# Where the gated-linear-attention levels, the weight folds of the first sub-block and the final norm stand among the projection matmuls of a one-core decoder step

## The chip, the core and the metric

The kernel runs on one core of a Trainium2 chip. The metric is the device time of one launch in microseconds (us); below it is better. The time before is 2868.98 us, the median of three runs between 2868.82 and 2869.27 us. The engines are called PE (matrix), PEld (its weight load), DVE (vector), ACT (scalar functions), POOL (GpSimd) and SP (which issues the DMAs).

## The reference, cut to what matters

One layer of a hybrid decoder is applied to a prompt of 2048 tokens of width 1024 and to 32 sample tokens (8 requests of 4), all in 32-bit floats:

```
q, k, v, r, a, u, sv = split(rmsnorm(x) @ w_in)
logg  = log_sigmoid(a @ w_alpha*rstd + b_alpha) / 16
o, S  = gated linear attention(q, k, v, logg)      # causal, per-channel decay exp(sum of logg)
o     = rmsnorm(o) * silu(r)
s_out = gelu(u) * (causal 128x128 mixing of rmsnorm(gelu(sv)))
h = x + concat(o, s_out) @ w_out
h = h + softmax attention over 256 memory tokens, wq_x and wo_x
y = h + conv_ffn(rmsnorm(h)); final rmsnorm
```

The outputs also hold the states, the memory keys and values and the convolution's last rows.

## The kernel before, in words

The prompt is cut into four sub-blocks of 512 tokens, called s = 0 to 3 here; the 32 sample tokens ride along in s = 1 for the mixer and in s = 2 for the FFN. A product of 32-bit matrices is made of three matmuls on halves that are rounded to a shorter type (`mm3`, lines 92 to 94): ACT makes the high half, DVE the rest (`split`, lines 84 and 85).

**The order of the work** is a list of steps that is written out by hand. `weave` goes through a main list and puts the steps of side lists between its members, spread evenly from a first to a last member. In a mixer the main list is: member 0 the small decay projection, 1 wk, 2 wq, 3 to 6 sv, 7 to 10 v, 11 and 12 u, 13 to 16 r, 17 and 18 the first two parts of w_out. Members 1, 2, 11 and 12 have 48 matmuls of 512 columns with two weight units, the members of sv, v and r 24 matmuls with one weight unit, the two of w_out 24 each. `run` walks the finished list and issues weight loads up to five units ahead of need, all on the SP queue, in the order of the list. The tile framework then orders the instructions of each engine at compile time, by their place in the list and by a simulated schedule; each engine runs its list strictly in that order.

**Marks** number the places between projection matmuls: eight in each 48-matmul member and four in each other one, so that marks 0 to 15 lie in wk and wq, 16 to 31 in sv, 32 to 47 in v, 48 to 63 in u and 64 to 79 in r. `behind(i)` keeps a group of PE instructions behind mark i on PE; it binds PE alone. `step_of(i)` gives the member that holds mark i, and the group's step stands behind that member in the list.

**The gated linear attention** works on two head pairs p = 0 and 1. `gates` (line 967 on) makes the log decays with three ACT functions from two table sets, `cums` sums them on PE. `diag(p)` makes the diagonal of the 128x128 score blocks (eight small ACT copies, line 1022). `level(p, l)`, l = 0 to 6, makes the off-diagonal blocks of size 2^l: DVE subtracts sums (line 1041), ACT takes Exp (lines 1043 and 1046), DVE multiplies with q and k (lines 1053 and 1057), PE makes the scores (line 1064) and DVE copies them in under a mask (line 1068). `decay(p)` and `states(p)` make the running state (line 1126 on PE), `chunks` the outputs (lines 1151 and 1152), `gate`, `times_r` (line 1166) and `back` (line 1223) finish them for w_out. The table `AT` holds the mark of each: levels stand three marks apart, from 18 for p = 0 and from 41 for p = 1.

**ACT** evacuates sv through Gelu (line 887), u through Gelu (line 873) and r through Silu (line 890). Gelu and Exp lie in different table sets, and a change of set is an instruction of its own (ACT_TABLE_LOAD in the profile). The four sv accumulators fill the four banks of the pool `accp`, and v's first matmul needs one of them back.

**The folds** stand in s = 0 alone. `turn_wq` loads 512 KB of wq_x, loads two tiles of a memory key again (`again`, line 585, from four buffers of the tag X, two per turn), transposes wq_x on PE (line 596) and splits it; `fold_qk` multiplies the two (24 matmuls of 256 columns), copies the result (line 619), splits it, makes sums (lines 632 to 635) and writes all of it to DRAM; the writes go onto the SP queue at the next fold (`flush`, line 301). There are eight pairs of turn and fold, 16 steps. `fold_vo` does the like for values and wo_x (8 steps of 12 matmuls of 512 columns, two for each of four heads, which share one reload). The tiles of all this come from the tag U, 49 buffers that the whole mixer shares.

**The final norm** of the sub-block before (`final_steps`, 4 parts, 5 after s = 2: transposes at line 1779, squares at 1780, result at 1786) stands at members 0 and 1 of the next mixer; after s = 2 six steps that write out the convolution rows (line 1797) stand there too.

Of the kernel before, what the change touches and what calls it, by code (L numbers as in the profile page):

```python
# [37 lines left out]
def hymba_step_kernel(  # L38
# [34 lines left out]
    def mps(name):  # L73
        return mmp.tile([128, 512], F32, tag="mm", name=name)
# [390 lines left out]
    def weave(main, *sides):  # L465

        out = []
        due = [0.0] * len(sides)
        at = [0] * len(sides)
        for i, m in enumerate(main):  # L470
            out.append(m)
            for j, (steps, first, last) in enumerate(sides):
                if i < first:
                    continue
                due[j] = len(steps) * min(1.0, (i - first + 1) / (last - first + 1))
                while at[j] < len(steps) and at[j] < due[j] - 1e-9:
                    out.append(steps[at[j]])
                    at[j] += 1
        for j, (steps, _, _) in enumerate(sides):
            out += steps[at[j]:]  # L480
        return out
# [182 lines left out]
    qk_steps = []  # L664
    for h, j in ((2 * i + hh, j) for i in range(2) for j in range(2) for hh in range(2)):
        qk_steps.append(Step(lambda a, h=h, j=j: turn_wq(h, j, a), [wraw_unit(wq_x[0], 4 * j, 4, h * 256, 256, f"wqf{h}{j}")]))
        qk_steps.append(Step(lambda h=h, j=j: fold_qk(h, j)))
    vo_steps = [Step(lambda a, h=h, jh=jh: fold_vo(h, jh, a), [(wo_x[0], 2 * h, 2, jh * 512, 512, f"wof{h}{jh}")])
                for h in range(4) for jh in range(2)]
# [5 lines left out]
    def behind(i):  # L675
        return tc.issue_after(marks[i])
# [227 lines left out]
    def sgu_steps(B):  # L904
# [21 lines left out]
        def mix(h):  # L926
# [22 lines left out]
        return [Step(f) for f in out]  # L949


    AT = {("diag", 0): 17, ("level", 0): 18, ("decay", 0): 39, ("states", 0): 50,
          ("diag", 1): 24, ("level", 1): 41, ("decay", 1): 62, ("states", 1): 66}
    state = {}
    for p in range(2):
        t = cp.tile([128, 128], F32, tag=f"S{p}", name=f"Sz{p}", bufs=2)
# [3 lines left out]
    def gla_steps(B):  # L960
        s, sample = B.s, B.mix_sample
        T = TM if sample else SB
        nt = 5 if sample else 4

        s0_of = {}

        def gates():
            if sample:
# [38 lines left out]
        def diag(p):  # L1007
# [3 lines left out]
            pool.tensor_tensor(pr[:, :T], B.q[p][:, :T], B.k[p][:, :T], ALU.mult)  # L1011
            with behind(AT["diag", p]):
                for c in range(nt):
# [13 lines left out]
        def level(p, l):  # L1027
            half = 1 << l
            Tl = TM if (sample and l < 2) else SB
            nb = Tl // (2 * half)  # L1030

            def lr(t):
                v = t[:, :Tl].rearrange("p (n two h) -> p n two h", two=2, h=half)
                return v[:, :, 0, :], v[:, :, 1, :]


            b3 = B.b[p][:, :Tl].rearrange("p (n w) -> p n w", w=2 * half)
            e = T_(f"e{s}{p}{l}")
            el, er = lr(e)
            if l > 0:  # L1040
                dve.tensor_tensor(e[:, :Tl].rearrange("p (n w) -> p n w", w=2 * half), b3,
                                  b3[:, :, half - 1:half].broadcast_to([128, nb, 2 * half]), ALU.subtract)
                act.activation(el, el, AF.Exp, scale=-1.0)
            else:
                dve.tensor_tensor(er, b3[:, :, 1:2], b3[:, :, 0:1], ALU.subtract)
            act.activation(er, er, AF.Exp)

            kr = T_(f"kr{s}{p}{l}")
            nr = Tl // 2
            kr3 = kr[:, :2 * nr].rearrange("p (hh i) -> p hh i", hh=2)  # L1050
            qr = lr(B.q[p])[1]
            for hh in range(2):
                dve.scalar_tensor_tensor(kr3[:, hh].rearrange("p (n h) -> p n h", h=half),
                                         er, sel[:, hh:hh + 1], qr, ALU.mult, ALU.mult)
            if l > 0:
                kl = e
                dve.tensor_tensor(el, el, lr(B.k[p])[0], ALU.mult)
            else:
                kl = B.k[p]
            ps = mps(f"s{s}{p}{l}")  # L1060
            ps3 = ps.rearrange("p (hh i) -> p hh i", hh=2)
            with behind(AT["level", p] + 3 * l):
                for c in range(4):
                    pe.matmul(ps3[:, :, c * 64:(c + 1) * 64], kl[:, c * 128:(c + 1) * 128],
                              kr3[:, :, c * 64:(c + 1) * 64], start=True, stop=True)
            for hh in range(2):
                dst = B.P[2 * p + hh][:, :SB].rearrange("p (n two h) -> p n two h", two=2, h=half)
                dve.copy_predicated(dst[:, :, 1, :], masks[l].rearrange("p (n h) -> p n h", h=half),
                                    ps3[:, hh].rearrange("p (n h) -> p n h", h=half))
            if sample and l < 2:  # L1070
                ps = mps(f"ss{s}{p}{l}")
                with behind(AT["level", p] + 3 * l):
                    pe.matmul(ps[:NS, :32].rearrange("p (hh i) -> p hh i", hh=2), kl[:, SB:TM], kr3[:, :, 256:272],
                              start=True, stop=True)
                for hh in range(2):
                    dst = B.P[2 * p + hh][:NS, SB:TM].rearrange("p (n two h) -> p n two h", two=2, h=half)
                    dve.copy_predicated(dst[:, :, 1, :], masks[l][:NS, :16].rearrange("p (n h) -> p n h", h=half),
                                        ps[:NS, hh * 16:(hh + 1) * 16].rearrange("p (n h) -> p n h", h=half))

        def decay(p):  # L1080
# [21 lines left out]
            ps = mps(f"ktp{s}{p}")  # L1102
            with behind(AT["decay", p]):
                for c in range(4):
# [4 lines left out]
            if sample:  # L1109
                ps = mps(f"ktps{s}{p}")  # L1110
                with behind(AT["decay", p]):
                    pe.transpose(ps[:NS, :128], kh[:, SB:TM], ident)
# [6 lines left out]
        def states(p):  # L1119

            kv = mps(f"kv{s}{p}")
            with behind(AT["states", p]):
              for c in range(4):
# [129 lines left out]
        put_at(1, lambda: cums(0), lambda: cums(1))  # L1253
        for p in range(2):
            todo = [(AT["diag", p], lambda p=p: diag(p))]
            todo += [(AT["level", p] + 3 * l, lambda p=p, l=l: level(p, l)) for l in range(7)]
            todo.append((AT["decay", p], lambda p=p: decay(p)))
            for i, f in sorted(todo, key=lambda x: x[0]):
                put_at(step_of(i), f)
# [552 lines left out]
    steps = [Step(mem_norm)]  # L1812
    norm = norm_in_steps(blocks[0])
    steps += weave(mem_steps, (norm, 0, 11), ([Step(late_constants)], 2, 2))
    after = []
    for s, B in enumerate(blocks):
        proj = proj_steps(B)
        gla = gla_steps(B)
        sgu_st = sgu_steps(B)
        nst = len(sgu_st) - 4  # L1820
        keep = None
        if B.mix_sample:
            def keep():
                if not hasattr(smp, "x"):
                    smp.x = U("smpx")
                return smp.x
        w1, w2, stat = out_proj_steps(B, lambda k0, m2, s=s: (w_out[0], k0, 4, m2 * 256, 256, f"wo{s}{k0}{m2}"),
                                      lambda B=B: B.cat, "gx", "wo", B.mix_sample, 4, B.mix_sample, keep, seven=True, whole=not B.mix_sample)
        folds = [(qk_steps, 8, 13), (vo_steps, 13, 17)] if s == 0 else []
        steps += weave(proj + w1, *folds, (after, 0, 1),  # L1830
                       *gla,
                       (sgu_st[:1], 6, 6), (sgu_st[1:nst], 7, 8), (sgu_st[nst:], 12, 13))
        scales, sc, turns = attention_steps(B)
        x1, x2, xstat = out_proj_steps(B, lambda k0, m2, s=s: wready(vod[k0 // 4][:, m2], f"wx{s}{k0}{m2}"),
                                       lambda B=B: B.ao, "gffn", "wx", False, 0, B.ffn_sample, seven=s > 0, whole=True)
        steps += w2 + [stat, scales]
        steps += weave(sc + x1, (turns[:2], 8, 9), (turns[2:3], 13, 13), (turns[3:], 14, 14))
        fstart, fmain, flast = ffn_steps(B, s == NSB - 1)
        steps += x2 + [xstat, fstart]
        sides = []  # L1840
        if B.mix_sample:
            sides.append((sample_steps(), 1, len(fmain) - 5))
        if s + 1 == NSB:
            ncs = conv_out_steps(carry, 2, o_state_conv[0, 0], "nc")
            sides.append((ncs[:4], 30, 36))
        steps += weave(fmain[:-4], *sides)
        if s + 1 < NSB:
            after = final_steps(B)
            nxt = blocks[s + 1]
            norm = norm_in_steps(nxt)  # L1850
            if nxt.ffn_sample:
                norm.append(carry_sample(nxt, B))
            steps += weave(fmain[-4:] + flast, (norm, 0, 4))
            if B.ffn_sample:
                after += conv_out_steps(sct, 16, o_state_conv_s[0].rearrange("b t f -> (b t) f"), "ncs")
        else:
            steps += fmain[-4:-2] + flast[:1] + fmain[-2:] + ncs[4:] + flast[1:]
            after = []
# [30 lines left out]
```

## Time and profile before

| what | value |
|---|---|
| median of three runs | 2868.98 us |
| profiled execution, device time | 2865.95 us |
| profiled execution, span from first to last instruction | 2864.2 us |
| PE busy | 2801.3 us, 98% |
| DVE, ACT, POOL busy | 1876.2, 1131.6, 564.4 us |
| mean granted PE clock | 0.992 |

The span is 1.75 us shorter than the device time of the same execution. A row of the windows view gives a stretch, its length, the busy time of each engine in it with the number of instructions, the granted PE clock, the share of the DMA engines and the rate. A row of the timeline gives start, duration, engine, line, operation and tiles, and in brackets the idle time before it with what ended it. A row of the waits gives who waited for whom, the total, how often and the longest one.

### The profile page before, as it was taken

To read this page: it belongs to the slowest core of one execution; us is meant where nothing else is said; L and a number is where in the kernel's file an instruction comes from. 1 tells how busy PE (TensorE), PEld (TensorE's weight loads), DVE (VectorE), ACT (ScalarE), POOL (GpSimd) and SP (SyncE) were. 2 spreads that over 40 slices of the span, in tenths; PEclk is the share of its full clock that TensorE was granted. 3 is DMA by queue.
4 is the path that set the end of the run, shared out by engine and by line. 5 is a ranking of instruction groups with operands and counts; after the bars stand their busy time and mean duration, and the time that the engine had idled before them with its cause. 6 is when DMAs were issued, how large, how long until landed. Compare 5 with 4: busy or idle time off the path is not lost.

```text
span 2864.2 us, 47088 instructions
## 1 busy us (share of the span) xinstructions
PE 2801.3 (98%) x17894; PEld 2478.0 (87%) x17894; DVE 1876.2 (66%) x3262; ACT 1131.6 (40%) x1971; POOL 564.4 (20%) x631
## 2 busy tenths in 40 slices
PE   8988999999999999999999999999999899999998
PEld 8777898888887788998888889899999788899997
DVE  6665768777776676655546767666666677665555
ACT  5544545333356344322224545422223545431222
POOL 2001212111101221321311121222221021132222
PEclk9999999999999999999999999999999999999999
DMA  9355779999952236887886225567776223677775
GB/s 300 108 181 177 272 239 327 338 341 341 319 192 91 82 111 236 299 290 277 315 311 220 81 74 192 201 247 258 258 265 212 86 76 131 215 255 267 272 276 180
DMA packets 369687, 638.21 MB, mean 223 GB/s; under 512 B 27370, under 2 KB 238412, under 8 KB 369462
## 3 DMA queue, kind: packets, MB, share of 16 engines
q1 hardware_dynamic: 369462, 635.20, 65.3%
q8 instruction: 142, 2.33, 0.3%
q14 instruction: 83, 0.68, 0.1%
HBM read 507.69 MB, written 127.41 MB: 222 GB/s over the span
## 4 chain that ended last, share of the span: by engine, by line
PE 87%; DVE 5%; ACT 3%; DMA 2%; issue 2%; POOL 1%; SPq 0%; POOLq 0%; ACTq 0%; DVEq 0%
PE d L92 6%; PE d L94 6%; PE d L93 6%; PE a_wx L92 2%; PE a_wx L94 2%; PE a_wx L93 2%; PE a_wo L92 2%; PE a_wo L93 2%; PE a_wo L94 2%; PE a_wg L94 1%; PE a_wup L94 1%; PE a_wg L92 1%; PE a_wup L93 1%; PE a_wup L92 1%; PE a_wg L93 1%
## 5 line engine op out<-in xcount | busy, mean ns | idle before, releaser
L92 PE MATMUL d<-acth,whi_wd 128*128 128x272 f32 (+1 forms) x688 | 235.6, 342 | 0.0
L94 PE MATMUL d<-acth,wlo_wd 128*128 128x272 f32 (+1 forms) x688 | 233.7, 340 | 0.0
L93 PE MATMUL d<-actl,whi_wd 128*128 128x272 f32 (+1 forms) x688 | 233.7, 340 | 0.0
L1738 DVE TENSOR_TENSOR h<-d,h 128x512 f32<-128x512 f32 (+1 forms) x232 | 133.9, 582 | 147.7 <-PE d L94 147.7
L1640 POOL TENSOR_TENSOR c<-c,bc_f 128x512 f32<-128x512 f32 (+1 forms) x88 | 137.1, 1562 | 138.8 <-ACT c L1639 138.1
L1630 ACT ACTIVATE c<-g,colsb 128x512 f32<-128x512 f32 x88 | 71.7, 815 | 204.5 <-DVE g L1599 154.5
L94 PEld LDWEIGHTS d<-acth,wlo_wd 128*128 128x128 f32 x688 | 129.3, 188 | 15.4 <-issue 1.2
L92 PEld LDWEIGHTS d<-acth,whi_wd 128*128 128x128 f32 x688 | 129.2, 188 | 15.3 <-DVE h L1738 1.7
L93 PEld LDWEIGHTS d<-actl,whi_wd 128*128 128x128 f32 x688 | 129.5, 188 | 13.9 <-issue 0.4
L1662 POOL TENSOR_TENSOR c<-r_q_wup,c 128x512 f32<-128x512 f32 (+1 forms) x33 | 62.7, 1900 | 335.7 <-DVE r_q_wup L286 213.7
L1627 POOL COPY carry<-g 128x2 f32<-128x2 f32 x88 | 30.9, 351 | 434.2 <-DVE g L1599 403.1
L92 PE MATMUL a_wo<-ch,h_wo 128*128 128x512 f32 (+1 forms) x320 | 112.5, 353 | 0.0
L93 PE MATMUL a_wo<-cl,h_wo 128*128 128x512 f32 (+1 forms) x320 | 112.3, 351 | 0.0
L94 PE MATMUL a_wo<-ch,l_wo 128*128 128x512 f32 (+1 forms) x320 | 112.2, 351 | 0.0
L1631 DVE SCALAR_TENSOR_TENSOR c<-g,colsb,c 128x512 f32<-128x512 f32 x88 | 86.1, 978 | 29.0 <-ACT c L1630 28.4
L94 PE MATMUL a_wx<-pTh,wlo_wx 128*128 128x512 f32 x256 | 101.2, 395 | 0.0
L84 ACT ACTIVATE acth<-c 128x512 fp32r<-128x512 f32 (+1 forms) x88 | 55.9, 636 | 113.6 <-DVE c L1662 84.6
L93 PE MATMUL a_wx<-pTl,whi_wx 128*128 128x512 f32 x256 | 100.5, 392 | 0.0
L92 PE MATMUL a_wx<-pTh,whi_wx 128*128 128x512 f32 x256 | 100.3, 394 | 0.0
L1639 ACT ACTIVATE c<-c 128x512 f32<-128x512 f32 (+1 forms) x88 | 56.1, 638 | 103.0 <-DVE c L1632 91.0
L1632 DVE SCALAR_TENSOR_TENSOR c<-g,colsb,c 128x512 f32<-128x512 f32 x88 | 92.7, 1054 | 1.1
L85 DVE TENSOR_TENSOR actl<-c,acth 128x512 fp32r<-128x512 f32 (+1 forms) x88 | 64.3, 733 | 27.2 <-ACT acth L84 26.0
(3757 smaller groups left out, 9731.9 us busy)
## 6 DMA issues: line engine op xcount, KB each, us to landing
whi_wd<-wd SPq DMA_DIRECT2D x66, 512.0 KB, 8.1
wlo_wd<-wd SPq DMA_DIRECT2D x66, 512.0 KB, 7.5
r_wo<-in_w_out_dram SPq DMA_DIRECT2D x32, 512.0 KB, 3.7
wlo_wx<-vod SPq DMA_DIRECT2D x32, 512.0 KB, 4.1
whi_wx<-vod SPq DMA_DIRECT2D x32, 512.0 KB, 5.0
r_wg<-in_w_gate_dram SPq DMA_DIRECT2D x22, 512.0 KB, 7.2
r_wup<-in_w_up_dram SPq DMA_DIRECT2D x22, 512.0 KB, 5.4
r_wd<-in_w_down_dram SPq DMA_DIRECT2D x22, 512.0 KB, 5.2
```

The costliest lines, as they stand in the source:

```text
L84: act.activation(hi, src, AF.Copy)
L85: (lo_eng or dve).tensor_tensor(lo, src, hi.bitcast(F32), ALU.subtract)
L92: pe.matmul(ps, wh, xh, start=first, stop=False)
L93: pe.matmul(ps, wh, xl, start=False, stop=False)
L94: return pe.matmul(ps, wl, xh, start=False, stop=last)
L1630: act.activation(c[:, :SB], g[:, 2:SB + 2], AF.Identity, bias=cb, scale=w2)
L1631: dve.scalar_tensor_tensor(c[:, :SB], g[:, 1:SB + 1], w1, c[:, :SB], ALU.mult, ALU.add)
L1632: dve.scalar_tensor_tensor(c[:, :SB], g[:, 0:SB], w0, c[:, :SB], ALU.mult, ALU.add)
L1639: act.activation(c[:, :T], c[:, :T], AF.Gelu_apprx_tanh)
L1640: pool.tensor_tensor(c[:, :T], c[:, :T], B.fbc[:, :T], ALU.mult)
L1662: (dve, pool)[i].tensor_tensor(c[:, :T], q[i], c[:, :T], ALU.mult)
L1738: dve.tensor_tensor(B.h[m + mm][:, cs], ps[:, :cw], B.h[m + mm][:, cs], ALU.add)
```

## The change

The table of marks becomes two tables, one for s = 0 and one for the other sub-blocks, with a mark of its own for each level. For s = 1 to 3 no level has a mark between 28 and 35 any more; the second pair's diagonal goes from mark 24 to 38 and its states from 66 to 69. For s = 0 all marks are later. The 16 steps of turns and folds of wq_x go from members 8 to 13 to members 0 to 9, the 8 steps for wo_x from 13 to 17 to 10 to 17. The final norm's steps stay at members 0 and 1, but stand behind the gates and the decay sums in the list; the convolution rows after s = 2 go to members 13 to 15.

```diff
-    AT = {("diag", 0): 17, ("level", 0): 18, ("decay", 0): 39, ("states", 0): 50,
-          ("diag", 1): 24, ("level", 1): 41, ("decay", 1): 62, ("states", 1): 66}
+    AT_FOLDS = {("diag", 0): 23, ("level", 0): (24, 27, 36, 39, 42, 45, 48), ("decay", 0): 51, ("states", 0): 56,
+                ("diag", 1): 46, ("level", 1): (52, 55, 58, 61, 64, 67, 70), ("decay", 1): 72, ("states", 1): 73}
+    AT_REST = {("diag", 0): 17, ("level", 0): (18, 21, 24, 27, 36, 38, 40), ("decay", 0): 43, ("states", 0): 50,
+               ("diag", 1): 38, ("level", 1): (45, 47, 50, 53, 56, 58, 61), ("decay", 1): 64, ("states", 1): 69}
...
+        AT = AT_REST if s else AT_FOLDS
...
-            with behind(AT["level", p] + 3 * l):
+            with behind(AT["level", p][l]):
...
-            todo += [(AT["level", p] + 3 * l, lambda p=p, l=l: level(p, l)) for l in range(7)]
+            todo += [(AT["level", p][l], lambda p=p, l=l: level(p, l)) for l in range(7)]
...
-        folds = [(qk_steps, 8, 13), (vo_steps, 13, 17)] if s == 0 else []
-        steps += weave(proj + w1, *folds, (after, 0, 1),
-                       *gla,
+        folds = [(qk_steps, 0, 9), (vo_steps, 10, 17)] if s == 0 else []
+        steps += weave(proj + w1, *folds, *gla, (after[:5], 0, 1), (after[5:], 13, 15),
                        (sgu_st[:1], 6, 6), (sgu_st[1:nst], 7, 8), (sgu_st[nst:], 12, 13))
```

More of the change, by code (lines that the diff above doesn't have):

```diff
@@ L1071, in level @@
                 ps = mps(f"ss{s}{p}{l}")
-                with behind(AT["level", p] + 3 * l):
+                with behind(AT["level", p][l]):
                     pe.matmul(ps[:NS, :32].rearrange("p (hh i) -> p hh i", hh=2), kl[:, SB:TM], kr3[:, :, 256:272],
```

## The prediction

> **What bounds the kernel now.** I read the page first, then the busy time of each engine by stretches, then PE's waits, then the timelines around the two largest.
>
> ```profile
> span 2864.2 us, 47088 instructions
> PE 2801.3 (98%) x17894; PEld 2478.0 (87%) x17894; DVE 1876.2 (66%) x3262; ACT 1131.6 (40%) x1971; POOL 564.4 (20%) x631
> PE 87%; DVE 5%; ACT 3%; DMA 2%; issue 2%; POOL 1%; SPq 0%; POOLq 0%; ACTq 0%; DVEq 0%
> ```
>
> PE is the bound: it sits idle for 2864.2 - 2801.3 = 62.9 us in all. The change adds and removes no matmul, so it can only win idle time and time at a lower clock. The windows say where these are (length, busy PE, PEld, DVE, ACT, POOL, granted clock, DMA share, GB/s):
>
> ```profile
> 76.00:150.00 74.00, 73.51 (x371) 59.67 (x372) 43.63 (x79) 45.54 (x99) 3.93 (x4) 1.00 0.28 87
> 150.00:200.00 50.00, 37.74 (x222) 33.28 (x221) 31.51 (x59) 16.77 (x31) 2.83 (x1) 0.86 0.61 195
> 200.00:240.00 40.00, 38.15 (x234) 32.64 (x233) 22.85 (x43) 16.79 (x27) 0.00 (x0) 1.00 0.54 173
> 240.00:300.00 60.00, 50.80 (x272) 42.94 (x271) 38.71 (x71) 27.27 (x43) 19.73 (x10) 0.89 0.68 223
> 300.00:370.00 70.00, 69.91 (x370) 59.23 (x370) 53.83 (x82) 41.05 (x64) 15.97 (x10) 1.00 0.67 236
> 815.00:1005.00 190.00, 187.32 (x1285) 153.58 (x1284) 130.02 (x276) 92.84 (x189) 32.45 (x27) 1.00 0.26 82
> 1549.00:1715.00 166.00, 164.01 (x891) 137.48 (x891) 112.81 (x200) 86.87 (x161) 26.34 (x19) 1.00 0.28 86
> 2260.00:2300.00 40.00, 32.34 (x164) 27.43 (x164) 29.11 (x58) 28.24 (x77) 5.69 (x3) 0.87 0.23 66
> 2300.00:2385.00 85.00, 85.00 (x479) 72.14 (x479) 57.18 (x98) 36.65 (x48) 17.05 (x11) 1.00 0.24 77
> ```
>
> The mixer of s = 0 (76 to 370) loses the most: 150 to 200 has 50 - 37.74 = 12.3 us idle and, at clock 0.86, up to 50 x 0.14 = 7.0 us of slow running; 240 to 300 has 9.2 us idle and up to 60 x 0.11 = 6.6 us; 200 to 240 has 1.9 us. In s = 3, 2260 to 2300 has 7.7 us idle and up to 40 x 0.13 = 5.2 us. The mixers of s = 1 and 2 lose only 2.7 and 2.0 us, with the clock at 1.00.
>
> What PE waited for in s = 0 (first three rows) and s = 3 (next two), and what the SP queue waited for in s = 0 (last two):
>
> ```profile
> PE qkp L92 <- ACT wqh L84: 12.4, 2, 8.6
> PE t_wr L92 <- ACT h_wr L84: 3.4, 1, 3.4
> PE a_wu L92 <- DVE v L868: 2.7, 1, 2.7
> PE t_wv L92 <- ACT sv L887: 5.7, 1, 5.7
> PE s L1064 <- DVE kr L1053: 1.9, 1, 1.9
> SPq L585 <- PE qkp L94: 47.1, 7, 9.4
> SPq L301 <- ACT qkh L84: 12.8, 5, 4.1
> ```
>
> Two waits of a fold for its split weights make up 12.4 of the 23.4 us that s = 0 loses. Why the split was late, on SP (first two rows) and ACT:
>
> ```profile
> 168.11 1.97 SPq L585 DMA_DIRECT2D kr<-kd  x2
> 170.17 0.38 SPq L102 DMA_DIRECT2D r_wu<-in_w_in_dram  x1
> 174.92 1.06 ACT L84 ACTIVATE h_wu<-r_wu 128x1024 fp32r<-128x1024 f32 x1 [3.44 <-DMA r_wu<-in_w_in_dram]
> 175.88 1.07 ACT L84 ACTIVATE wqh<-wqp 128x512 fp32r<-128x512 f32 x2
> ```
>
> The load of r_wu stands on SP behind the reload of a memory key (line 585), which waits for a fold's last matmul to free its X buffer; ACT runs in order, waits for r_wu, and the fold's split stands behind it. So the folds hold up the projection's loads, and the projection's splits the folds.
>
> In s = 3, on ACT (first four rows) and PE:
>
> ```profile
> 2274.28 2.45 ACT L1022 ACTIVATE P<-ident,dgs 128x128 f32<-128x128 f32 x8 [1.15 <-DVE dgs L1016]
> 2276.73 1.28 ACT L887 ACT_TABLE_LOAD   x1
> 2278.03 2.42 ACT L887 ACTIVATE sv<-t_ws,xrs 128x512 f32<-128x512 f32 x4
> 2280.47 1.28 ACT L1043 ACT_TABLE_LOAD   x1
> 2267.91 0.40 PE L94 MATMUL t_ws<-h_ws,xl 128*128 128x512 f32 x1
> 2278.77 0.80 PE L92 MATMUL t_wv<-h_wv,xh 128*128 128x512 f32 x1 [5.73 <-ACT sv L887]
> 2283.40 0.43 PE t_wv L93
> 2284.13 0.23 PE t_wv L92
> ```
>
> PE finished sv at 2268.3; ACT reached sv's Gelu at 2278.0, behind the second pair's diagonal (2.45 us) and a chain of Exps. After the gap PE steps at 0.43 us a matmul until about 2284, then at 0.23.
>
> **The change part by part.** *Places that leave out sv's Gelu, and gates first (s = 3).* From before the Gelu go the second diagonal (eight copies, 2.45 us of ACT) and three levels, whose scores now stand at marks 36 to 40. One level costs DVE
>
> ```profile
> L1053 DVE SCALAR_TENSOR_TENSOR kr<-e,sel,q 128x256 f32<-128x256 f32 (+1 forms) x112 | 49.3, 480 | 2.4 <-ACT e L1046 2.3
> L1041 DVE TENSOR_TENSOR e<-b 128x512 f32<-128x512 f32 (+1 forms) x48 | 33.3, 695 | 0.0
> L1068 DVE COPY_PREDICATED P<-mask,s 128x256 f32<-128x256 uint8 x112 | 52.6, 525 | 27.7 <-PE s L1064 25.7 <-PE t_ws1q L725 0.7 <-ACT P L1022 0.6
> ```
>
> 2 x 0.480 + 0.695 + 2 x 0.525 = 2.7 us of DVE, so 8.1 us for three. The delay from 2268.3 to 2278.0 is 9.7 us, and 2.45 + 8.1 = 10.6 covers it. The decay sums come earlier as well, since the final norm's transposes and six convolution rows no longer stand ahead of them. Those six steps go to r's members, where 2300 to 2385 leaves DVE 28 and ACT 48 us free: I cost them at nothing; without that room each is one DVE copy of about the size of a 128x512 step above, 6 x 0.695 = 4.2 us. What is late next is the score's own wait of 1.9 us. I take 10 of the 7.7 + 5.2 = 12.9 us; bounds 0 (Exps still issue first) and 12.9.
>
> *s = 1 and 2.* Only 4.7 us is there to win. Against it, the second pair's states move from mark 66 to 69, which puts them behind member 15 in place of 14: 24 matmuls of 0.23, 5.5 us later. In s = 3 the end of that chain reads:
>
> ```profile
> 2354.21 1.02 PE kv L1126 x16
> 2372.45 0.75 DVE L1166 TENSOR_TENSOR o<-o,r 128x256 f32<-128x256 f32 x2
> 2375.72 1.75 PE otp L1223 x16
> ```
>
> The last product with r is done at 2373.2, 2.5 us before the transposes of line 1223 start; the second part of w_out (24 matmuls, 5.5 us) still follows these. Slack 2.5 + 5.5 less about 3 us of splits is 5 us, against 5.5: I take 0 for these; bounds -3 x 5.5 = -16.5 (for s = 1 to 3) and +4.7.
>
> *Folds at members 0 to 9 (s = 0).* All that a pair issues moves: a weight load, two reloads, six writes on average on SP; eight transposes and 24 matmuls; on ACT about 3.3 us (two splits 1.07, by the row at 175.88, two copies and two more splits of that size), on DVE as much. Eight pairs put some 26 us on ACT and on DVE into members 0 to 9. From 76 to 150 ACT has 28 and DVE 30 us free, POOL 70, the DMA share is 0.28, and levels leave that stretch. Between a fold and the reload that takes over its buffer stand two members now in place of one: at least 5.5 us of PE more, against a mean wait on line 585 of 47.1 / 7 = 6.7 us. So the wait that held r_wu shrinks to about 1 us, and I take the 19.3 us of 150 to 200 as gone. Against it: the first reload is issued while the loads and writes of the memory stage still run, and the trace has no fold there. Its bound is 0 below and 8.6 above, the longest wait of a fold; I take 3, since the queue is light soon after 76. A gain is excluded: nothing waits there now.
>
> *Folds of wo_x at 10 to 17, levels later.* The 15.8 us of 240 to 300 lose the other half of the qk folds (4 of its 9.2 idle), but the second pair's seven levels now lie in u and r (marks 52 to 70), with Gelu and Exp taking turns as they do today. I take half, 7.9; bounds 0 and 15.8. The second pair's states come after r; today, too, they come after it, and the folds and w_out cover them without loss (300 to 370 has 0.1 us idle). With most folds gone from there the cover is 2 x 5.5 us of w_out and one or two folds of 12 x 0.23 = 2.8 us, some 15 us, against 2373.2 - 2354.2 = 19 us of chain: I take 3 us lost; bounds 0 and 10.
>
> Sum: 10 + 0 + 19.3 - 3 + 7.9 - 3 = 31 us. The profiled execution took 2865.95 us, 3.0 us below the median of the runs; 2865.95 - 31 = 2835 there, and 2868.98 - 31 = 2838 as a median.
>
> The Trainium skill (TensorE: Matmul & The Clock Gate, Part 1) says the clock is halved after an idle window of about 3.4 us and comes back after as long a busy one. By that each gap costs an estimated 1.7 us beside its idle time; with two long gaps in s = 0 and one in s = 3 the clock's share would be 5.1 us, where my sum takes some 14 of the 18.8 that the clock column bounds; the sum would be 9 us smaller, 2847. The trace shows half speed from 2278.8 to 2284, 5.2 us and 2.4 us lost, more than the page's figure. The Trainium skill (ScalarE: Activation LUTs, What ACT_TABLE_LOAD costs) gives 2.66 us for a change of table with its drain; here sv starts 1.30 us after the load does, so the trace disagrees, and each change saved is worth half of that.
>
> **The rivals.** *The stall only moves within s = 0.* The folds' buffers and vo's writes are short again beside v, u and r, and s = 0 keeps what it loses but 3 us, with s = 3 paying as above: 2868.98 - 13 = 2856. For it: SP waits on splits as well (12.8 us at line 301). Against: DMA and ACT are light from 76 to 150.
>
> *The edit does not do what it says.* `behind` binds PE; the subtractions and Exps of the late levels are free to issue early, and the compile-time order may put them ahead of the Gelu as before. Then s = 3 keeps its 12.9 us: 2868.98 - 21 = 2848. Against: the diagonal and its copies sit behind a PE mark, and they go.
>
> *Slower: the queue in front of the projection.* A reload that waits holds up the loads of wq and sv, five units ahead at most, and those come one every 5.5 us. If the wait of a reload exceeds two members' work, PE stops as at 176: 8.6 us and 2.4 us of slow running, 11 us a time. Five such stops of eight make 55 us, against 35.1 + 12.9 = 48 that could be won: 2876. It decides from the point where a fold ends more than 11 us after its turn's place. For it: today seven of the reloads wait, up to 9.4 us. Against: that is under 11.
>
> **How the numbers follow.** The forecast gets 0.58, the moved stall 0.15, the unchanged order 0.14, the slower case 0.13. A difference of 0.2%, 5.7 us, is about what a measurement of this kernel can tell from no change. The forecast's own range, with the ends of its terms, is 2820 to 2852; the low end is 49 us, nearly all of the 35.1 + 12.9 us. With the two milder rivals and the edge of the slower one it is 2820 to 2866. Faster by over 0.2%: the first three cases, less some 0.05 for a moved stall that eats s = 3 as well: 0.82. Within 0.2%: that 0.05 and a little of the slower case, 0.06. Slower: 0.12.
>
> **What would show it.** Right: the waits of the fold for its split fall from 12.4 to under 4 us; the clock of s = 0 is 1.00 throughout; the wait of t_wv for sv in s = 3 is under 1 us, and the second diagonal's copies lie behind sv's Gelu; line 585's wait falls well below 47 us. Wrong: PE idles over 3 us before 110, at the join of v and u, or between r and w_out in s = 0, or between the first two parts of w_out and the rest in s = 1 to 3.

## The result, and the profile after

The changed kernel takes 2852.14 us (median of four runs, 2847.66 to 2853.19), the kernel before 2868.9 us on the same chips (2865.12 to 2869.27): a ratio of 0.9942, 95% interval 0.9924 to 0.9959, 16.8 us faster. The forecast was 31 us, to 2838. The profiled execution of the change is the slowest of its four, 2853.19 us; between the two traces the span falls by 12.7 us, and the accounts by stage below add up to that.

The page of the changed kernel, its span and its engines:

```profile
span 2851.5 us, 47065 instructions
PE 2803.3 (98%) x17894; PEld 2479.6 (87%) x17894; DVE 1889.7 (66%) x3262; ACT 1135.7 (40%) x1975; POOL 565.4 (20%) x631
```

PE has the same 17894 matmuls; its idle time falls from 62.9 to 2851.5 - 2803.3 = 48.2 us. The windows of the change, s = 0 (five rows), the join of v and u in s = 1, and the end of sv in s = 3 (length, busy PE, PEld, DVE, ACT, POOL, clock, DMA share, GB/s):

```profile
76.00:150.00 74.00, 71.21 (x399) 59.59 (x400) 45.23 (x82) 38.44 (x67) 1.29 (x1) 0.98 0.66 214
150.00:200.00 50.00, 46.66 (x278) 40.81 (x278) 34.44 (x68) 32.38 (x76) 6.01 (x3) 0.99 0.72 223
200.00:240.00 40.00, 39.66 (x229) 33.60 (x228) 31.71 (x57) 22.00 (x34) 0.00 (x0) 1.00 0.59 194
240.00:300.00 60.00, 59.78 (x316) 49.79 (x315) 49.25 (x74) 29.40 (x44) 17.26 (x11) 1.00 0.63 206
300.00:370.00 70.00, 68.61 (x459) 62.75 (x458) 54.73 (x93) 37.48 (x68) 14.38 (x9) 1.00 0.57 190
880.00:905.00 25.00, 18.08 (x90) 13.84 (x89) 21.71 (x43) 10.18 (x23) 3.58 (x2) 0.87 0.27 88
2260.00:2300.00 40.00, 39.40 (x202) 33.01 (x201) 28.77 (x51) 24.23 (x54) 4.21 (x2) 1.00 0.23 67
```

In s = 0 PE idles 8.1 us between 76 and 370 where it idled 23.9, and the clock is 0.98 to 1.00 where it was 0.86 and 0.89. The stop of s = 3 is gone. But s = 1 has a new one: 6.9 us idle in 25 us, clock 0.87.

PE's waits in the change, s = 0 (first row), s = 1 (next three), s = 2 and 3 together (the fifth), and the reloads of memory keys on SP in s = 0 (last):

```profile
PE qkp L92 <- ACT wqh L84: 2.8, 1, 2.8
PE s L1068 <- DVE kr L1057: 3.2, 2, 2.6
PE s L1068 <- DVE km L1119: 2.3, 1, 2.3
PE ss L1077 <- DVE kt L1111: 1.4, 1, 1.4
PE a_wo L92 <- ACT r L890: 4.0, 2, 2.1
SPq L585 <- PE qkp L94: 33.7, 8, 9.8
```

The wait of a fold for its split falls from 12.4 to 2.8 us, the wait of v for sv in s = 3 from 5.7 to nothing. New are 6.9 us of score matmuls that wait for DVE in s = 1, and 4.0 us of w_out's first matmul waiting for r's Silu. The reloads on SP still wait 33.7 us (47.1 before), although one fold alone still stops PE: that does not fit my account of the stop. ACT's waits for the folds' writes q7p, 17.4 us in four waits in s = 0 before, are gone.

ACT at the end of sv in s = 3:

```profile
2254.48 0.40 ACT L1050 ACTIVATE e<-e 128x256 f32<-128x256 f32 x1
2254.90 1.28 ACT L887 ACT_TABLE_LOAD   x1
2256.20 0.69 ACT L887 ACTIVATE sv<-t_ws,xrs 128x512 f32<-128x512 f32 x1
2259.94 1.28 ACT L1047 ACT_TABLE_LOAD   x1
2263.22 1.28 ACT L887 ACT_TABLE_LOAD   x1
```

The Gelu starts at 2256, while PE is still in sv (v starts at 2258.96). An Exp still cuts in, with two table loads, and costs PE nothing. The second diagonal's copies are gone from here.

The one wait of a fold that is left, on PE (first row) and ACT:

```profile
146.28 0.39 PE L92 MATMUL qkp<-kr,wqh 128*128 128x256 f32 x1 [2.79 <-ACT wqh L84]
142.35 1.06 ACT L84 ACTIVATE h_wv<-r_wv 128x1024 fp32r<-128x1024 f32 x1 [1.98 <-DMA r_wv<-in_w_in_dram]
143.32 2.43 ACT L1026 ACTIVATE P<-ident,dgs 128x128 f32<-128x128 f32 x8
145.65 0.57 ACT L84 ACTIVATE wqh<-wqp 128x512 fp32r<-128x512 f32 x1
```

It is the fifth fold, not the first: the first starts at 92.2, and PE is busy for all of 76 to 110. Its split stands on ACT behind a projection's split that waits for its load, and behind the first pair's diagonal.

Where the time goes, as the start of a stage's first matmul in each profile against before (us; minus is earlier). "Scores" is the first score matmul of the memory attention, which follows the mixer:

| place | before | change | e1_folds | e2_rest | e3_norm | e5_folds_norm | e13_wtag |
|---|---|---|---|---|---|---|---|
| scores, s = 0 | 356.1 | -26.3 | -25.7 | -4.6 | -1.0 | -24.9 | -27.8 |
| mixer, s = 1 | 817.3 | -23.0 | -21.0 | -2.1 | -0.9 | -21.5 | -26.0 |
| scores, s = 1 | 1053.3 | -12.2 | -19.1 | +8.6 | -0.8 | -21.3 | -25.8 |
| mixer, s = 2 | 1548.9 | -11.5 | -17.4 | +8.8 | -0.3 | -20.9 | -23.1 |
| scores, s = 2 | 1745.8 | -8.4 | -17.4 | +11.2 | +0.8 | -19.6 | -22.8 |
| mixer, s = 3 | 2196.1 | -7.7 | -16.1 | +12.5 | +1.2 | -20.4 | -22.9 |
| first v matmul, s = 3 | 2278.8 | -19.8 | -16.1 | +1.9 | -8.7 | -30.3 | -22.9 |
| scores, s = 3 | 2416.1 | -13.3 | -15.8 | +10.8 | -6.7 | -28.5 | -22.9 |
| end | 2864.2 | -12.8 | -15.0 | +11.6 | -7.1 | -28.9 | -22.9 |

These are single executions, and a stage that an edit leaves alone moves by 1 to 5 us from one to the next (s = 0 in e2_rest). In the change s = 0 wins 26.3 us, the mixer of s = 1 loses 10.8, that of s = 2 loses 3.1, and s = 3 wins 12.1 up to v and gives 6.5 back behind it.

### The profile page after: what moved, and what is told of

Its sections match the earlier page's. It is cut to its first block, busy times and chain, and to the rows that moved or that the text cites. A ratio compares the mean times of both kernels' runs of the same rounds, so it can differ in the third digit from the quotient of the medians.

```text
span 2851.5 us, 47065 instructions
## 1 busy us (share of the span) xinstructions
PE 2803.3 (98%) x17894; PEld 2479.6 (87%) x17894; DVE 1889.7 (66%) x3262; ACT 1135.7 (40%) x1975; POOL 565.4 (20%) x631
```

## The experiments

All ratios are against the kernel before on the same chip, with a 95% interval. In the diffs AT_OLD is the old table, written out level by level.

**The three parts alone.** The first sub-block's marks and folds:

```diff
-        AT = AT_REST if s else AT_FOLDS
+        AT = AT_OLD if s else AT_FOLDS
-        steps += weave(proj + w1, *folds, *gla, (after[:5], 0, 1), (after[5:], 13, 15),
+        steps += weave(proj + w1, *folds, (after, 0, 1), *gla,
```

> Only the parts of the first sub-block: its later table of marks and its folds at members 0 to 9 and 10 to 17; the other sub-blocks and the final norm stand as before. Between the two traces the first score matmul of s = 0 comes 26.3 us earlier and the mixer of s = 1 starts 23.0 us earlier. Theory A (the three parts add up, and the places of s = 1 to 3 cost more than they win): 23 us faster, 2846. Rival B (the folds' gain is only there because the gates of the next sub-block come earlier, or half of it is given back in the FFN of s = 0, which runs at a DMA share of 1.0): 2855 or more.

Measured: 2851.02 us, 0.9944 (0.9931 to 0.9958), about 16 us faster. The 23 us of theory A were not reached. Rival B's half is not given back in the FFN, where -25.7 becomes -21.0 at the next mixer; by the end of this one profile 10.7 of the 25.7 us are gone, 6 of them in sub-blocks that the edit leaves alone. The folds' part alone wins as much as the whole change.

The places of s = 1 to 3:

```diff
-        AT = AT_REST if s else AT_FOLDS
+        AT = AT_REST if s else AT_OLD
-        folds = [(qk_steps, 0, 9), (vo_steps, 10, 17)] if s == 0 else []
+        folds = [(qk_steps, 8, 13), (vo_steps, 13, 17)] if s == 0 else []
-        steps += weave(proj + w1, *folds, *gla, (after[:5], 0, 1), (after[5:], 13, 15),
+        steps += weave(proj + w1, *folds, (after, 0, 1), *gla,
```

> Only the new table of marks for s = 1 to 3; first sub-block, folds and final norm as before. Theory A: s = 1 loses about 11 us between v and u because the levels that left marks 28 to 35 crowd marks 36 to 47 and PE waits in order for their products, s = 2 and 3 lose 2 us each where the first w_out matmul waits for r's Silu, and s = 3 wins some 10 at sv's Gelu: 2869 + 15 - 10 = 2874. Rival B (s = 1 loses by the order of the final norm, not by the places): no loss in s = 1, 2860.

Measured: 2875.02 us, 1.0019 (1.001 to 1.0028), 5 us slower, as theory A had it. By the table the mixer of s = 1 loses 10.7 us and that of s = 2 loses 2.4, and s = 3 wins 10.6 up to v, of which 8.9 are gone by the scores.

The order at the start of the mixers:

```diff
-        AT = AT_REST if s else AT_FOLDS
+        AT = AT_OLD
-        folds = [(qk_steps, 0, 9), (vo_steps, 10, 17)] if s == 0 else []
+        folds = [(qk_steps, 8, 13), (vo_steps, 13, 17)] if s == 0 else []
```

> Only the order at the start of the mixers of s = 1 to 3: gates and decay sums ahead of the final norm, the convolution rows at members 13 to 15; all marks and the folds as before. Theory A: the decay sums come some 30 us earlier against v in s = 3, the Exps are done before sv ends, and most of the wait of 5.7 us with its slow running goes with this part alone: 2869 - 8 = 2861; s = 1 unchanged. Rival B: s = 1 loses its 11 us here, and s = 3 keeps its wait, since the second diagonal still stands ahead of the Gelu: 2875 to 2880.

Measured: 2858.35 us, 0.9967 (0.9954 to 0.9979), about 9 us faster. In s = 3 the old places, with the second diagonal still at mark 24, win 9.9 us up to v once the decay sums come first. PE's waits of v for sv in this kernel, all of s = 1 to 3:

```profile
PE t_wv L92 <- ACT sv L887: 0.7, 2, 0.3
```

So earlier decay sums are enough to take the stop away, and the diagonal and the three levels did not need to move. The places are nearly enough too: in e2_rest, where the sums come as late as before, v waits 1.8 us for sv in s = 3 in place of 5.7. It took late sums together with the old places to make the stop. The three parts add up to -0.0056 + 0.0019 - 0.0033 = -0.0070, against -0.0058 for the whole, within the intervals.

**Where s = 1 loses.** The changed kernel with the old table in s = 1:

```diff
-        AT = AT_REST if s else AT_FOLDS
+        AT = AT_FOLDS if s == 0 else AT_OLD if s == 1 else AT_REST
```

> The changed kernel, but s = 1 with the old table of marks. Theory A: the 7.4 us of PE waits at v's end in s = 1 and their slow running go, 11 us faster than the changed kernel, 2841. Rival B: s = 1 keeps its loss, 2852.

Measured: 2844.22 us, 0.9917 (0.9904 to 0.9931); the interval overlaps that of the change (0.9924 to 0.9959) at its edge. The profiles are clearer: here the mixer of s = 1 loses 0.2 us (-19.5 at its start, -19.3 at the scores), in the change 10.8. Then only the first pair at its old places:

```diff
-        AT = AT_REST if s else AT_FOLDS
+        AT = AT_FOLDS if s == 0 else AT_S1 if s == 1 else AT_REST
+    AT_S1 = {("diag", 0): 17, ("level", 0): (18, 21, 24, 27, 30, 33, 36), ("decay", 0): 39, ("states", 0): 50,
+             ("diag", 1): 38, ("level", 1): (45, 47, 50, 53, 56, 58, 61), ("decay", 1): 64, ("states", 1): 69}
```

> The changed kernel, but in s = 1 the first pair's levels and decay stand at the old marks (18 to 36 and 39); the second pair keeps the changed places. Theory A (marks 36 to 47 are crowded: three levels, a decay, a diagonal and the next pair's first levels want DVE within three members): with three levels out of there, the waits of the score matmuls at v's end fall from 7.4 to under 3 us, 6 us or more faster than the changed kernel, 2846. Rival F (the second pair's first levels at 45 and 47 are themselves too early behind v's evacuation): no change in s = 1, 2852.

Measured: 2844.53 us, 0.9927 (0.9911 to 0.9944). The interval overlaps that of the change by half, so the times alone do not tell the two apart; the profiles do. The mixer of s = 1 loses 0.8 us here (-20.7 to -19.9), 10.8 in the change, and 8.1 in e8_states66 below, whose first pair stands as in the change. The v stage of s = 1 in this kernel (first row) and in the change (second row):

```profile
857.00:893.00 36.00, 35.96 (x174) 26.40 (x173) 24.16 (x52) 26.79 (x73) 9.43 (x5) 1.00 0.44 135
860.00:896.00 36.00, 31.97 (x159) 23.41 (x155) 20.49 (x39) 23.82 (x69) 10.24 (x4) 1.00 0.39 121
```

PE is idle for 0.04 us where it is idle for 4.03, and the score matmuls no longer wait there. The second pair's places are the same in both, so it is the first pair's three levels and its decay, moved into marks 36 to 43, that crowd DVE in v. The marks bind PE in order: a score matmul that stands at its mark and waits for DVE holds up the projection behind it. Why the same places cost 10.8 us in s = 1 and only 3.1 in s = 2 is not shown; s = 1 alone carries the sample tokens.

**The tail of the second pair.**

```diff
-               ("diag", 1): 38, ("level", 1): (45, 47, 50, 53, 56, 58, 61), ("decay", 1): 64, ("states", 1): 69}
+               ("diag", 1): 38, ("level", 1): (45, 47, 50, 53, 56, 58, 61), ("decay", 1): 64, ("states", 1): 66}
```

> The changed kernel with the second pair's states back at mark 66 for s = 1 to 3, so that its step stands behind member 14 again; all else as changed. Theory A (the chain of the second pair ends one member later, and r's Silu stands on ACT behind its first square, so w_out's first matmul waits 2.1 us in s = 2 and s = 3): these 4 us go and s = 1's end gets earlier too, 5 us faster than the changed kernel, 2847. Rival H (the decay at 64 and the levels up to 61 already set that chain): no change, 2852.

Measured: 2851.67 us, 0.9949 (0.9936 to 0.9963): the same as the change. w_out's wait for r's Silu in s = 2 and 3 goes from 4.0 to 3.0 us:

```profile
PE a_wo L92 <- ACT r L890: 3.0, 2, 1.9
```

Theory A fails here: the place of the states is not what makes the tail late. Which of the levels and the decay does was not tried.

**Without the new places.**

```diff
-        AT = AT_REST if s else AT_FOLDS
+        AT = AT_OLD if s else AT_FOLDS
```

> The changed kernel without the new places of s = 1 to 3, which keep the old table of marks; folds, first sub-block's table and the order of the final norm as in the change. Theory A (the places of s = 1 to 3 cost, the other two parts add up): -17.8 - 10.4 = 28 us faster than before, 2841, and faster than the changed kernel by 11. Rival C (the places are needed beside the new order, and s = 1 alone loses by them): no better than the changed kernel with s = 1 on the old table, 2844 or more.

Measured: 2841.5 us, 0.9916 (0.99 to 0.9931). Its interval overlaps that of the change (0.9924 to 0.9959) at its edge. Its profile is 16 us shorter, but shows the fastest of its six executions, and that of the change the slowest of four. It is no worse than the change with s = 1 on the old table, so the places are not needed anywhere.

**What stopped the folds.** Only the folds moved, all marks old:

```diff
-        AT = AT_REST if s else AT_FOLDS
+        AT = AT_OLD
-        steps += weave(proj + w1, *folds, *gla, (after[:5], 0, 1), (after[5:], 13, 15),
+        steps += weave(proj + w1, *folds, (after, 0, 1), *gla,
```

> Only the folds move to members 0 to 9 and 10 to 17; every sub-block keeps the old table of marks, so that in s = 0 the first pair's levels meet the folds; final norm as before. Theory A (the folds' move is what frees PE, since reloads and writes no longer stand beside the loads of u and r): most of the 17.8 us stay, 2856 or less. Rival D (the later marks do it, because levels and folds would share DVE, ACT and the tag U in sv and v): half is lost or more, 2860 to 2875, with sv's Gelu late in s = 0.

Measured: 2848.69 us, 0.9938 (0.9923 to 0.9952), as much as with the later marks. sv's Gelu is late in s = 0, as rival D says, and PE waits for it:

```profile
PE t_wv L92 <- ACT sv L887: 5.2, 1, 5.2
```

Yet the total is the same: the marks of s = 0 shift stops and win nothing in sum.

The kernel before with half the reloads:

```diff
-        again("k", h)
+        if j == 0:
+            again("k", h)
+            mem_st.t["k", h] = mem_st.t["k"]
...
-        kh, kl = mem_st.t["k"]
+        kh, kl = mem_st.t["k", h]
```

> The kernel before with one edit: a memory key is loaded again only for the first of its two turns and held for the second, so that 8 of the 16 reload DMAs go, and with them the reloads that wait for a fold's last matmul to free their buffer in the middle of a head. Folds, marks and norm as before. Theory A (the reload at the head of the SP queue holds r_wu, ACT waits for it in order, and the fold's split behind it): the stop of 8.6 us and about 2.4 us of slow running go, 11 us faster, 2858. Rival E (the folds wait for buffers of the tag U that their DRAM writes hold): under 3 us, 2866 or more.

Measured: 2861.27 us, 0.9981 (0.9969 to 0.9992), 5 us, half of what theory A said. The folds' wait for their split is still 10.0 us, and ACT's is on writes (line 84, waits in s = 0 of this kernel; the last row is the kernel before):

```profile
PE qkp L92 <- ACT wqh L84: 10.0, 2, 6.2
ACT wqh L84 <- DMA q7p<-qkh: 7.0, 3, 4.3
ACT wqh L84 <- DMA q7p<-qkh: 6.4, 2, 3.6
```

The 10.0 us are two waits, as before. The stop of 8.6 us is one of 6.2 here, so the reload was worth 2.4 us of it; at this stop ACT now waits 0.96 and 0.38 us for writes before the split. The other wait, 3.8 us, is the same in both kernels, and neither a reload nor a write makes it. There the split stands on ACT behind a step of the mixing that waits for POOL (kernel before):

```profile
267.71 0.63 ACT L84 ACTIVATE ch<-z 128x512 fp32r<-128x512 f32 x1 [5.68 <-POOL z L943]
```

The split and what the writes carry share the tag U, so a write that ends a wait of a split is taken to be one that frees its buffer. In the kernel before, the splits that waited for a write (at 191.5 and 230.2) are not the two that PE waited for. I then issued the writes at the end of their own fold:

```diff
                 put(sums[:, 2 * i:2 * i + 2, jj], t[:, :512].rearrange("p (s m) -> p s m", s=2))
+        flush()
```

> The kernel before with one edit: a fold's writes to DRAM are put on the SP queue at the end of that fold, not at the start of the next one. Reloads, folds' members, marks and norm as before. In the trace before ACT waits 17.5 us in four waits for writes q7p that hold buffers of the tag U, and with the reloads halved it still waits 17.8. Theory E (buffers of the tag U held by writes stop the folds): the waits fall to half or less and s = 0 ends 5 to 10 us earlier, 2856 to 2861. Rival G (SP runs in order: writes put on earlier wait there for their splits and hold the loads of u and r behind them): the waits change from writes to loads, within 3 us of before or slower.

Measured: 2865.08 us, 0.9998 (0.999 to 1.0007). It tells nothing either way: in both profiles a write is issued 0.2 us (median) after what it writes is ready, and lands 4.1 us later. There was hardly a delay to take away. So I gave the split other buffers:

```diff
-            hi, lo = U(f"wqh{h}{j}{dt}", F32R), U(f"wql{h}{j}{dt}", F32R)
-            split(hi[:, :512], lo[:, :512], ps)
+            if dt == 0:
+                wth = wp.tile([128, 2, 512], F32R, tag="whi", name=f"wqh{h}{j}")
+                wtl = wp.tile([128, 2, 512], F32R, tag="wlo", name=f"wql{h}{j}")
+            hi, lo = wth[:, dt], wtl[:, dt]
+            split(hi, lo, ps)
```

> The kernel before with one edit: the split, transposed wq_x of a fold lives in the weight tiles' tags whi and wlo in place of four buffers of the tag U a pair; members, reloads, marks and norm as before. Theory E (in s = 0 the folds at members 8 to 13 run out of buffers of the tag U, so that ACT waits 17.5 us for the landing of writes, and PE for ACT): with four to eight buffers more for the folds, those waits fall to under 9 us and s = 0 ends 8 us earlier or more, 2858 or less. Rival (the reloads and the loads behind them would stop the folds at the same places anyway, or the weight tiles are now what is short): within 3 us of before, 2863 or more.

Measured: 2844.47 us, 0.9924 (0.9912 to 0.9936), 22 us faster than before with every step where it was. PE's waits for folds and ACT's longest wait in s = 0, and the two windows that held the stops:

```profile
PE qkp L92 <- ACT wqh L84: 1.0, 3, 0.5
ACT qkf L622 <- DMA q7p<-qkl: 8.2, 2, 4.7
150.00:200.00 50.00, 44.90 (x275) 38.68 (x274) 40.47 (x76) 21.58 (x41) 0.04 (x1) 1.00 0.75 247
240.00:300.00 60.00, 60.00 (x316) 50.31 (x316) 42.13 (x66) 32.65 (x48) 11.03 (x8) 1.00 0.97 335
```

The window from 240 is full, at clock 1.00. Not all went as expected: ACT still waits 8.2 us in one kind of copy alone, and 11.0 us for all writes q7p (17.4 before), not under 9. But the split that PE waits for no longer does. The edit also changes the order of ACT's instructions, which is made at compile time. In the kernel before, two of u's splits (165.67 and 174.92) stand between those of the second fold (160.17) and the third (175.88). Here one does, and the first half of the third fold's split stands ahead of the next:

```profile
158.34 1.05 ACT L84 ACTIVATE h_wu<-r_wu 128x1024 fp32r<-128x1024 f32 x1
167.22 0.60 ACT L84 ACTIVATE wqh<-wqp 128x512 fp32r<-128x512 f32 x1 [0.35 <-PE wqp L596]
167.71 1.05 ACT L84 ACTIVATE h_wu<-r_wu 128x1024 fp32r<-128x1024 f32 x1
```

The eighth fold's split, too, stands ahead of the step that waits for POOL (238.85 and 239.82), where it stood behind it. That buffers of its own for the split take the stops away is shown; how much of the 22 us comes from waits for writes and how much from this order is not. One edit on buffers wins at least what the move of the steps wins. The buffers together with the earlier decay sums were not tried.

Last, the version of e5_folds_norm with half the reloads:

```diff
-        AT = AT_REST if s else AT_FOLDS
+        AT = AT_OLD if s else AT_FOLDS
-        again("k", h)
+        if j == 0:
+            again("k", h)
+            mem_st.t["k", h] = mem_st.t["k"]
...
-        kh, kl = mem_st.t["k"]
+        kh, kl = mem_st.t["k", h]
```

> The change without its places for s = 1 to 3, as in the fifth experiment, and a memory key is loaded again only once for its two turns. Theory A and E: the reloads still wait 33.7 us on SP in the changed kernel, but no fold waits for a write there, and what a fold loses is 2.8 us: 0 to 4 us faster than the fifth experiment's 0.9916 of before, 2837 to 2841. Rival: the held key keeps two more X buffers taken, the next heads' reloads wait longer: slower than the fifth by 3 us or more.

Measured: 2844.02 us, 0.992 (0.9908 to 0.9933), not different from e5_folds_norm: with the folds at members 0 to 9 the reloads cost nothing that can be measured.

## Why the prediction was right or wrong, point by point

The sign was right, and the sum was 14 us too large. The 2852.14 us lie at the upper end of the forecast's own range (2820 to 2852) and inside the one with the rivals (to 2866). The number alone speaks for no case: two rivals, 2848 and 2856, lie nearer to it than the forecast's 2838. The traces decide.

**Folds of s = 0**: 21.2 us were forecast (19.3 + 7.9 - 3 - 3), 26.3 came at the scores and 23.0 at the next mixer. By parts: the first fold was to cost 3 us and cost none; that the fifth waits 2.8 us, about the same, is chance. 240 to 300 gave all but 0.2 of its 9.2 us of idle time, not half. The tail behind r was to cost 3 us, but PE is busy without a gap from 300 to the scores at 329.8; the 1.4 us idle in 300 to 370 are two waits of the scores themselves. That the size held is partly luck, since the cause holds only in part. "The folds hold up the projection's loads" made the reload on SP the stop. Halving the reloads took 2.4 of the stop's 8.6 us and won 5 us in all, the change left 33.7 us of reloads waiting almost without harm, and 22 us came from the edit on buffers alone. The step that failed is the reading of the chain at 168 to 176: I followed the load of r_wu, the last thing that ACT waited for, and did not ask why the fold's split stood behind it. With buffers of its own its first half stands ahead. Whether waits for writes or the place on ACT weighs more stays open. The 12.4 us were also read as one case, and the second wait, 3.8 us, came from a split that stood on ACT behind a wait for POOL. The rival that named the buffers had the right resource; its guess that it would stay short beside u and r did not come true.

**Sub-blocks s = 1 and 2**: taken as 0, they lost 10.8 and 3.1 us in the profile. This is the largest part of the miss. The term's lower bound, -16.5 for s = 1 to 3, covers it by luck: it was the price of another mechanism. The step priced one cost of the new places, the states one member later, and experiment e8_states66 shows that this one cannot be measured. What the step left out: three levels and a decay moved from marks 30 to 39 to marks 36 to 43, into a stretch that already holds the scaling of sv, the splits of u's weights and v's evacuation. I used the 2.7 us of DVE for a level where they left, and not where they arrived.

**s = 3**: 10 us were forecast; 12.1 came up to v, and 6.5 were given back. e3_norm, with the old places, gives back 2.0: that is about the moved convolution rows, 2.9 us of PE time that only changed their place. The other 4.5 go with the places: e5_folds_norm, which lacks only these, gives back 1.8. The 10.6 us that I credited to leaving out the Gelu were not needed, since earlier decay sums alone won 9.9; the sum took the two as one gain, and either alone wins nearly all of it (10.6 in e2_rest). The rival of an unchanged order was half right on ACT, where an Exp still cuts in, and wrong on the time.

**Slower**: five stops were priced, and PE has at most one short stop of this kind, the 2.8 us at 146.3. The reloads of keys waited up to 9.8 us, under the 11 that I gave as the point. A reload of values waited 12.5 us, over it, and PE did not stop: its longest gap between 156 and 329.8 is 1.0 us.

**The clock**: from 76 to the first score matmul PE has the same work in both kernels (before, then change):

```profile
76.00:356.10 280.10, 256.30 (x1348) 214.17 (x1349) 180.65 (x314) 140.19 (x252) 38.59 (x21) 0.95 0.55 181
76.00:329.80 253.80, 247.12 (x1349) 208.14 (x1350) 184.33 (x311) 139.43 (x250) 35.26 (x21) 0.99 0.62 199
```

Idle time falls from 23.8 to 6.7 us, so it gives 17.1 of the 26.3 us, and the other 9.2 come from the clock and the pace after gaps. The windows' bound for these was 13.6 us. I counted two long gaps in s = 0; the trace has three of 3.4 us or more (8.6, 3.8 and 3.4). By the Trainium skill (TensorE: Matmul & The Clock Gate, Part 1) the two long gaps would have been worth an estimated 3.4, and three 5.1; the measurement decides.

**The signs**: the fold's wait, v's wait for sv in s = 3 and the place of the second diagonal came as forecast. The clock of s = 0 was not 1.00 throughout (0.98 in 76 to 150), and line 585 waits 33.7 us for keys and, newly, 13.8 for values. None of the wrong signs came: the list has the join of v and u for s = 0, and the loss came there in s = 1.

## What to carry to other kernels

When an in-order engine waits for a DMA, list everything that the next instruction waits for, its output buffer too; the last of these to end is not the only one, and taking it away uncovers the next. Ask too why the instruction stands behind the one that waits. When steps are moved, add up the engine's work where they arrive as well as where they leave: a matmul pinned to a place in PE's order turns a late vector product into a stop of the whole projection. And try each part of a combined change alone: here one of three cost time, and the other two together (0.9916) did at least as well without it.

## What the runs showed of the hardware that was not expected

After the gap of 5.7 us in s = 3 of the kernel before, matmuls took 0.43 us in place of 0.23 for some 5 us, so a gap costs more than its length; in s = 0 the change won 26.3 us where only 17.1 us was idle time. A gap of 2.8 us was enough (granted clock 0.97 in 110 to 150), and the slow pace did not start at once: in the change matmuls of 256 columns stepped at 0.12 us right after the gap that ended at 146.28, and at 0.21 us from 149.25 to 150.53. A change of table on ACT cost 1.30 us from its start to the start of the next function again (2254.90 to 2256.20).
